# Mixers at 0.25 steps per unit of feed-forward work, and decode rows' second feed-forward products with unsplit weights, in a one-core hybrid decoder layer

## The chip, the cores and the metric

The kernel runs on one core of one Trainium2 chip. The metric is the device time of one execution in microseconds (us). A change of 0.3% of this time is about 8.5 us.

## The reference, cut to what matters

One decoder layer is computed for 2048 prompt rows and for 8 decode rows (one new token of each of 8 sequences), with the same weights. The width is 1024 and the feed-forward width 4096, all in float32.

```
proj = x @ w_in                                   # 1024 -> 3336 columns
o_r  = rwkv7_mix(proj[..., :1792] with token shift)   # recurrent over rows
o_m  = mamba2_mix(rest of proj)                       # scan over chunks of rows
h    = layer_norm(ALPHA * x + concat(o_r, o_m) @ w_out)
ff   = square(relu(h @ w_ff1)) @ w_ff2
y    = layer_norm(ALPHA * h + ff)
```

Besides y, the recurrent states after the last row are returned. What the change touches is the product with `w_ff2` for the 8 decode rows, and when the two mixers (`o_r`, `o_m`) of a block of prompt rows are worked on.

## The kernel before

The prompt is cut into four blocks of 512 rows. Nothing of the mixers of a block can start before its projection, and the output projection of a block needs the block's mixer output `s_o`, which goes through device memory. The 8 decode rows ride along with block 1 (`sblk`).

**Precision.** Large products are not done in plain float32. Each operand is split in two (`split`): ScalarE writes a rounded high part, VectorE (at some places GpSimd) the rest, and `mm3` does three products (high by high, high by low, low by high) of the type `float32r`, lines L166 to L168. Weights come in pieces of 128x512 floats by `wpiece`: a DMA on the SP queue (L205) into a raw buffer of the pool `wr` (7 buffers), then the split into a buffer of the pool `w` (8 buffers). Small products, `mm` at L152, are often done on plain float32 operands; one such product appears in the trace as two matmul instructions.

**Stages.** First the projections of blocks 0 to 3 (`project`), with the mixers of block 0 as filling work at `RATE_M0`. Then `tail(b)` for each block: output projection (16 steps, each yielding 2.6 units), layer norm and transposes, then eight groups of feed-forward work. A group is four calls of `ff1` (24 matmuls of 512 columns each, yielding 5.2 units; they run four ahead of their group, `LA`) and eight second products (12 matmuls each, yielding 2.6). In the last group, `before_last` first finishes whatever filling work is left, then loads `s_o` of block b+1 (`load_o`, L323), its residual rows (L1289, into tiles of the pool `g4`) and the `w_out` pieces, and runs the whole output projection of block b+1; only after that come the second products of the last group.

**Filling work.** `drive` runs a tail and, for every unit that the tail yields, credits the mixers of the next block with `rate` steps; each full credit runs one step of the generator `mixers`, whose work takes 71 steps. From the first `ff1` to the point where the last group starts, a tail yields 32 x 5.2 + 7 x 20.8 = 312 units. `tail(0)` carries the mixers of block 1 and then the decode rows' own mixer work (`sample`) at `RATE_S`; `tail(1)` and `tail(2)` carry the mixers of blocks 2 and 3 at `RATE_M`; `tail(3)` carries none. The last three steps of `mixers` contain the end of `rwkv_post` for the last 128 rows: `inv_root` (step 69), whose four products write 32 output partitions each of one PSUM tile; a round trip of the result through device memory (`bcast_rs`, L552 and L554); the load of `s_bv` (L785); a product with `gup`; and the store of `s_o` (L798) in step 71.

**Order.** The program gives every instruction its buffers and a rank in order of the text above; a list scheduler then fixes one order per engine and for the SP queue, and the engines run it strictly in that order. So a DMA issue on SP that waits for a buffer holds up those behind it.

**Decode rows in the second product.** In `tail(1)`, each of the 8 groups has two halves of 512 output columns. When a half's four weight pieces are loaded, the eight decode rows' products are done first: `hid[f][2]` holds the high and the low part of the hidden values side by side, 16 columns, and eight `float32r` products (four pieces, high and low weight part) accumulate in 16 partitions of one PSUM bank. ScalarE copies them out (L1415) and VectorE adds them to rows 64 to 79 of the tile `hs[4]` (L1416). At the end `fold16` adds high and low rows by a small product.

Of the kernel before, what the change touches and what calls it, by code (L numbers as in the profile page):

```python
# [9 lines left out]
F32 = mybir.dt.float32  # L10
F32R = mybir.dt.float32r
I32 = mybir.dt.int32
AF = mybir.ActivationFunctionType
ALU = mybir.AluOpType
# [9 lines left out]
LA = 4  # L24

TURN = (0, 0, 0, 0, 2, 2, 2, 2)
RATE_M0, RATE_M, RATE_S = 0.2, 0.23, 0.35
BUFS = (("wr", 7), ("w", 8), ("act", 8), ("g4", 13), ("r", 2), ("blk", 4),
        ("m2", 3), ("q2", 2), ("m4", 2), ("ms", 1), ("lr", 1), ("sc", 2), ("ar", 2), ("bk", 1), ("xs", 3),
        ("xf", 1), ("uv", 2), ("bt", 1), ("st", 2), ("r1", 1), ("hids", 8))  # L30
D = 1024
# [2 lines left out]
NS = 8  # L34
# [34 lines left out]
_n = 0  # L69
for _name, _w in (  # L70
    ("ident", 128), ("scm", 128), ("m1", 64), ("m2", 64), ("bm", 4), ("d16", 16), ("tri", 128),
    ("b64", 128), ("cen", 128), ("s16", 8), ("sel", 32), ("one", 2),
):
    CCOL[_name] = (_n, _w)
    _n += _w
# [3 lines left out]
def shape_constants():  # L79
    c = np.zeros((128, NCON), np.float32)  # L80

    def put(name, v):
        o, w = CCOL[name]
        c[:, o:o + w] = v

    p = np.arange(128)
    s = p % 64
    t = np.arange(64)
    put("ident", np.eye(128))
    scm = np.zeros((128, 128))  # L90
    scm[:, :64] = s[:, None] < t[None, :]
    scm[:, 64:] = s[:, None] <= t[None, :]
    put("scm", scm)
    tb, sb = s // 16, t // 16
    put("m1", (tb[:, None] % 2 == 1) & (sb[None, :] == tb[:, None] - 1))
    put("m2", (tb[:, None] >= 2) & (sb[None, :] < 2))
    put("bm", tb[:, None] == np.arange(4)[None, :])
    put("d16", (p % 16)[:, None] == np.arange(16)[None, :])
    put("tri", p[:, None] <= p[None, :])
    blk = (p[:, None] // 64) == (p[None, :] // 64)  # L100
    put("b64", blk)
    put("cen", np.eye(128) - blk / 64.0)
    put("s16", p[:, None] % 8 == np.arange(8)[None, :])
    put("sel", (p[:, None] // 64) == (np.arange(32) % 2)[None, :])
    put("one", 1.0)
    return c


class K:
# [88 lines left out]
        nc.scalar.activation(hi, raw, AF.Copy)  # L198
        (eng or nc.vector).tensor_tensor(out=lo, in0=raw, in1=hi.bitcast(F32), op=ALU.subtract)  # L199

    def wpiece(self, src, shape, tag="w"):

        n = int(np.prod(shape))
        raw = self.sb(tag + "r", (128, 512))
        self.nc.sync.dma_start(raw[:, :n], src)  # L205
        hl = self.sb(tag, (128, 2, 512), F32R)
        self.npiece += 1
        r = {"a": POOLA, "o": POOLO, "f": POOLF}[self.pf]
        pool = r and self.npiece % r == 0
        self.split(raw[:, :n], hl[:, 0, :n], hl[:, 1, :n], self.nc.gpsimd if pool else None)  # L210
        return [hl[:, i, :n].rearrange("p (a b) -> p a b", a=shape[0]) for i in range(2)]
# [20 lines left out]
    def setup_mix(self):  # L232

        tc, nc, A = self.tc, self.nc, self.A
# [48 lines left out]
        c = lambda n, s: self.mp.tile(list(s), F32, name=n)  # L283

        self.wup = []
        for i in range(2):
            raw = self.sb("wr", (128, 512))
# [14 lines left out]
        self.hist = c("hist", (128, 8, 3))  # L302
        nc.gpsimd.memset(self.hist, 0.0)
        self.prl = c("prl", (128, 14))
        self.cen = self.mp.tile([128, 128], F32R, name="cen")
        nc.scalar.activation(self.cen, self.con("cen"), AF.Copy)
        self.b64 = self.mp.tile([128, 128], F32R, name="b64")
        nc.scalar.activation(self.b64, self.con("b64"), AF.Copy)
        self.hst = c("hst", (128, 8, 64))
        nc.gpsimd.memset(self.hst, 0.0)  # L310
        self.ST = self.sb("st", (128, 4, 64))
# [220 lines left out]
    def inv_root(self, groups, ones, scale, eps, clip=False):  # L532


        nc = self.nc
        n = 32 * len(groups)
        pss = self.ps("a" if clip else "m", (128, 128))
        for g, x in enumerate(groups):
            self.mm(pss[32 * g:32 * g + 32, :], ones, x)
        ss, y, t = (self.smp.tile([128, 128], F32, tag=x, name=self.nm(x), bufs=2)[:n] for x in ("rss", "rsy", "rst"))  # L540
        if clip:
            nc.vector.tensor_scalar(out=ss, in0=pss[:n], scalar1=eps, scalar2=None, op0=ALU.max)
        else:
            nc.vector.tensor_scalar(out=ss, in0=pss[:n], scalar1=scale, scalar2=eps, op0=ALU.mult, op1=ALU.add)
        return self.rsqrt(ss, 128, n, (y, t))
# [390 lines left out]
    def sample(self):  # L936
        self.pf = "s"
        nc, A = self.nc, self.A
# [36 lines left out]
        w = V6[:, 1]  # L975
# [18 lines left out]
        tt(sq, kk, kk, M)  # L994
        yield
        pn = self.ps("m", (128, 32))
        self.mm(pn, self.con("b64"), f(sq))
        ss = t(32)
        nc.vector.tensor_scalar(out=ss, in0=pn, scalar1=1e-24, scalar2=None, op0=ALU.max)
        rs = self.rsqrt(ss, 32)  # L1000
# [8 lines left out]
        rk = t(4, 8)  # L1009
# [1 line left out]
        tt(rk, rk, V6[:, 2], M)  # L1011
        yield
        pb = self.ps("m", (128, 32))
        self.mm(pb, self.con("b64"), f(rk))
        bv = t(4, 8)
        tt(bv, pb.rearrange("p (a b) -> p a b", a=4), v, M)

# [63 lines left out]
        y = yield from from_rows(yq)  # L1081
        yield
        pc = self.ps("m", (128, 32))
        self.mm(pc, self.con("cen"), f(y))
        nc.vector.tensor_copy(f(y), pc)
        tt(sq, y, y, M)
        yield
        pv = self.ps("m", (128, 32))
        self.mm(pv, self.con("b64"), f(sq))
        ts(ss, pv, 1.0 / 64, LNX_EPS)  # L1090
        tt(f(y), f(y), self.rsqrt(ss, 32), M)
        tt(y, y, bc("lnw", 4, 8), M)
# [155 lines left out]
                nc.vector.scalar_tensor_tensor(out=h[:, s], in0=h[:, s], scalar=rs, in1=b, op0=ALU.mult, op1=ALU.add)  # L1248
            nc.sync.dma_start(out[:, s], h[:, s])

    def ln_s(self, xs):

        bs = self.sm("bss", [128, 2, 6], bufs=1)[0:8]
        self.fold16(xs)
        for q in range(2):
            self.stats(xs[0:8], bs, q)
        yield from self.ln([xs[0:8]], [bs], 8)

    def fold16(self, xs):

        s16, x = xs[64:80], xs[0:8]
        for q in range(2):
            p = self.ps("b")
            self.mm(p[0:8, :], self.con("s16", 64, 80), s16[:, q * 512:(q + 1) * 512])
            self.nc.vector.scalar_tensor_tensor(out=x[:, q * 512:(q + 1) * 512], in0=x[:, q * 512:(q + 1) * 512],
                                                scalar=ALPHA, in1=p[0:8, :], op0=ALU.mult, op1=ALU.add)

# [11 lines left out]
    def tail(self, b, act, before_last):  # L1279
# [42 lines left out]
                    if kh:  # L1322
                        nc.scalar.activation(xs[64:80, ds_], pss[4][0:16], AF.Copy)
        if smp:
            for _ in self.ln_s(xs):
                pass
        yield 0

# [42 lines left out]
        for g in range(NFT // 4):  # L1371
# [23 lines left out]
            for j, (dh, i) in enumerate(order):  # L1395
                if last and nxt is not None:
                    self.pf = "o"
                    for _ in range(TURN[j]):
                        next(nxt)
                    self.pf = "f"  # L1400
                ds_ = slice(dh * 512, dh * 512 + 512)
                if len(w2s) == dh:
                    w2 = [self.wpiece(A["w_ff2"][f * 128:(f + 1) * 128, ds_], (1, 512)) for f in range(4 * g, 4 * g + 4)]
                    w2s.append(w2)
                    if smp:
                        ps = self.bank()
                        for f in range(4):
                            for s in range(2):
                                self.mm(ps[0:16], hid[f][2], w2[f][s][:, 0, :], f == 0 and s == 0, f == 3 and s == 1)
                        s16 = hs[4][64:80, ds_]  # L1410
                        if g == 0:
                            nc.scalar.activation(s16, ps[0:16], AF.Copy)
                        else:
                            t16 = self.sb("r", (128, 512))[64:80]
                            nc.scalar.activation(t16, ps[0:16], AF.Copy)  # L1415
                            nc.vector.tensor_tensor(out=s16, in0=t16, in1=s16, op=ALU.add)  # L1416
                w2 = w2s[dh]
                ps = self.bank()
                for f in range(4):
                    l = [hid[f][0][:, s, i * 128:(i + 1) * 128] for s in range(2)]  # L1420
                    r = [w2[f][s][:, 0, :] for s in range(2)]
                    self.mm3(ps, l, r, f == 0, f == 3)
                self.accum(hs[i][:, ds_], ps, g == 0)
                if last:
                    self.stats(hs[i], bs[:, i], dh)
                    if nxt is None and dh == 1:
                        if i == 0:
                            ab = self.affine(2)
                        self.norm(hs[i], bs[:, i], ab, rows[i], POOLN[i])
                yield 2.6  # L1430

        def finish():
            if nxt is not None:
                ab = self.affine(2)
                yield from self.ln(hs[:4], [bs[:, i] for i in range(4)], 128)
                for i in range(4):
                    yield from self.gain(hs[i], 128, *ab, rows[i])
            if smp:
                yield from self.ln_s(hs[4])
                yield from self.gain(hs[4][0:8], 8, *ab, A["y_s"])  # L1440

        if nxt is not None:
# [3 lines left out]
    def ff1(self, f, hT, segs, hid=None):  # L1446
# [6 lines left out]
        for o, m in segs:  # L1453
# [8 lines left out]
            c = min(m, TB - o)  # L1462
            self.split(rl[:, :c], hl[:, 0, o:o + c], hl[:, 1, o:o + c])
            if c < m:
                hid[2] = self.sb("hids", (128, 2 * NS), F32R)
                self.split(rl[:, c:m], hid[2][:, 0:NS], hid[2][:, NS:2 * NS])
        return hid


# [88 lines left out]
def layouts(x):  # L1558
# [2 lines left out]
    g = {n: np.asarray(a) for n, a in x.items()}  # L1561
    d = {}
    d["consts"] = shape_constants()

    def cols(name, tiles=None):
        a = g[name].reshape(-1)
# [66 lines left out]
```

## Time and profile before

| | |
|---|---|
| median of 3 runs | 2832.1 us (2827.39 to 2836.89) |
| the profiled execution's own time | 2837.96 us |
| its span, first to last instruction | 2836.1 us |
| mean granted TensorE clock | 0.983 |
| busy share: TensorE matmul, VectorE, ScalarE, GpSimd | 97%, 70%, 44%, 10% |

A busy share is an average over stages. TensorE is the engine that the kernel keeps busy, and its idle time and its clock are what the following rows look at: the busy time of each engine in a stretch, the clock that was granted there, and the chain of instructions that ended last.

### The profile page before, as it was taken

The numbers are of one execution on the slowest core, as the hardware profiler recorded it, in microseconds if no ns is written. First come the engines' busy times: TensorE is split into PE (matmuls) and PEld (weight loads), VectorE is DVE, ScalarE is ACT, GpSimd is POOL, SyncE is SP. The second block draws the span as 40 slices with busy tenths as digits, with TensorE's granted clock in tenths as the row PEclk, the third lists the DMA queues.
The fourth block names the chain that finished last, engine by engine and source line by source line (L and its number), as shares of the span: only waits on it lengthen the run. The fifth ranks groups of instructions, "written<-read, shape, count | busy, mean of one in ns | idle before, by whom it ended". The sixth has DMA issues, their size and how long they took to land.

```text
span 2836.1 us, 49575 instructions
## 1 busy us (share of the span) xinstructions
PE 2739.1 (97%) x17978; PEld 2211.4 (78%) x17978; DVE 1990.6 (70%) x4733; ACT 1246.6 (44%) x2376; POOL 297.0 (10%) x468
## 2 busy tenths in 40 slices
PE   9999999899999999999999999989999997999997
PEld 7788887677776777877888888867777775888886
DVE  7878979868868777774886666558776764664446
ACT  5554544445525443343644444326343332543332
POOL 2222222122210000001000000010000001000001
PEclk9999999999999999999999999989999998999999
DMA  6654655555633444354443343163444334342332
GB/s 203 185 181 138 182 174 143 167 169 166 184 116 121 143 134 136 105 158 155 134 136 113 106 125 114 57 198 130 121 127 127 115 97 139 98 149 88 98 97 71
DMA packets 326841, 382.79 MB, mean 135 GB/s; under 512 B 84222, under 2 KB 190292, under 8 KB 326588
## 3 DMA queue, kind: packets, MB, share of 16 engines
q1 hardware_dynamic: 326596, 379.63, 44.3%
q8 instruction: 141, 2.31, 0.3%
q14 instruction: 104, 0.85, 0.1%
HBM read 318.76 MB, written 60.81 MB: 134 GB/s over the span
## 4 chain that ended last, share of the span: by engine, by line
PE 66%; DVE 5%; DMA 3%; issue 1%; ACT 1%; SPq 0%; POOL 0%; DVEq 0%; ACTq 0%; POOLq 0%
PE psb L166 14%; PE psb L167 14%; PE psb L168 14%; PE psm L152 5%; PE psa L166 4%; PE psa L167 4%; PE psa L168 4%; PE psc L152 2%; PE psm L173 1%; PE psy L751 1%; PE psb L152 1%; DMA wr<-in_w_out_dram 1%; DMA q<-s_bv 0%; DMA g<-in_ln_g_dram 0%; DVE g L1228 0%
## 5 line engine op out<-in xcount | busy, mean ns | idle before, releaser
L198 ACT ACTIVATE w<-wr 128x512 fp32r<-128x512 f32 x788 | 485.5, 626 | 637.9 <-PE psb L168 396.2
L199 DVE TENSOR_TENSOR w<-wr,w 128x512 fp32r<-128x512 f32 x704 | 491.3, 705 | 252.9 <-ACT w L198 248.9
L166 PE MATMUL psb<-act,w 128*128 128x512 f32 (+2 forms) x1688 | 612.4, 363 | 6.8 <-ACT act L198 5.8
L167 PE MATMUL psb<-act,w 128*128 128x512 f32 (+2 forms) x1688 | 605.9, 359 | 0.0
L168 PE MATMUL psb<-act,w 128*128 128x512 f32 (+2 forms) x1688 | 603.3, 357 | 2.1 <-DVE w L199 2.1
L166 PEld LDWEIGHTS psb<-act,w 128*128 128x128 f32 x1688 | 319.6, 189 | 60.1 <-ACT act L198 5.8
L168 PEld LDWEIGHTS psb<-act,w 128*128 128x128 f32 x1688 | 319.2, 189 | 51.3 <-DVE w L199 2.5
L167 PEld LDWEIGHTS psb<-act,w 128*128 128x128 f32 x1688 | 320.0, 190 | 47.0 <-DVE act L199 0.9
L166 PE MATMUL psb<-w,g 128*128 128x512 f32 x768 | 310.0, 404 | 1.0 <-DVE g L1510 1.0
L167 PE MATMUL psb<-w,g 128*128 128x512 f32 x768 | 305.5, 398 | 0.0
L168 PE MATMUL psb<-w,g 128*128 128x512 f32 x768 | 304.6, 397 | 0.0
L1510 DVE TENSOR_TENSOR g<-psb,g 128x512 f32<-128x512 f32 x168 | 115.4, 687 | 104.2 <-PE psb L168 103.8
L166 PEld LDWEIGHTS psb<-w,g 128*128 128x128 f32 x768 | 144.7, 188 | 38.7 <-issue 2.0
L199 POOL TENSOR_TENSOR w<-wr,w 128x512 fp32r<-128x512 f32 x84 | 118.3, 1409 | 538.8 <-ACT w L198 256.4
L168 PEld LDWEIGHTS psb<-w,g 128*128 128x128 f32 x768 | 144.8, 189 | 33.7 <-issue 0.2
L167 PEld LDWEIGHTS psb<-w,g 128*128 128x128 f32 x768 | 144.9, 189 | 32.2 <-issue 0.4
L1460 ACT ACTIVATE r<-psb 128x512 f32<-128x512 f32 (+2 forms) x120 | 61.6, 513 | 182.2 <-PE psb L168 180.4
L199 DVE TENSOR_TENSOR g<-r,g 128x512 fp32r<-128x512 f32 (+1 forms) x160 | 92.5, 579 | 57.1 <-ACT g L198 56.7
L166 PE MATMUL psa<-act,w 128*128 128x512 f32 (+1 forms) x320 | 114.1, 357 | 0.0
L167 PE MATMUL psa<-act,w 128*128 128x512 f32 (+1 forms) x320 | 112.6, 352 | 0.0
L168 PE MATMUL psa<-act,w 128*128 128x512 f32 (+1 forms) x320 | 112.4, 351 | 0.0
L166 PE MATMUL psb<-g,w 128*128 128x256 f32 (+2 forms) x312 | 105.4, 338 | 0.3 <-ACT g L578 0.3
(380 smaller groups left out, 4886.2 us busy)
## 6 DMA issues: line engine op xcount, KB each, us to landing
wr<-in_w_ff_dram SPq DMA_DIRECT2D x512, 256.0 KB
wr<-in_w_in_dram SPq DMA_DIRECT2D x208, 256.0 KB
lr<-d_l SPq DMA_DIRECT2D x256, 64.0 KB
wr<-in_w_out_dram SPq DMA_DIRECT2D x64, 256.0 KB
s_m<-g SPq DMA_DIRECT2D x48, 256.0 KB
ms<-s_m SPq DMA_DIRECT2D x16, 768.0 KB
wr<-in_xT_dram SPq DMA_DIRECT2D x32, 256.0 KB
s_ar<-g SPq DMA_DIRECT2D x16, 512.0 KB
```

Source lines behind the costliest of these rows:

```text
L152: return self.nc.tensor.matmul(out, l, r, start=start, stop=stop)
L166: nc.tensor.matmul(out, l[0], r[0], start=first, stop=False)
L167: nc.tensor.matmul(out, l[0], r[1], start=False, stop=False)
L168: nc.tensor.matmul(out, l[1], r[0], start=False, stop=last)
L173: self.nc.tensor.transpose(out, in_, self.cst[p0:p0 + k, o + p0:o + p0 + k])
L198: nc.scalar.activation(hi, raw, AF.Copy)
L199: (eng or nc.vector).tensor_tensor(out=lo, in0=raw, in1=hi.bitcast(F32), op=ALU.subtract)
L751: acc = lambda o, l, r, start, stop: nc.tensor.matmul(o, l, r, start=start, stop=stop, skip_group_check=True)
L1460: nc.scalar.activation(rl, ps, AF.Relu)
L1510: self.nc.vector.tensor_tensor(out=h, in0=ps, in1=h, op=ALU.add)
```

## The change

Five things are edited.

1. `RATE_M` goes from 0.23 to 0.25, so the mixers of blocks 2 and 3 get a step every 4 units of feed-forward work in `tail(1)` and `tail(2)`.
2. The decode rows' second products use the raw float32 weights (`raws`) and plain float32 hidden values (32 columns, of which 8 are filled and 24 are zero). The four products of a half write the four groups of 32 partitions of one PSUM bank, without accumulation. The raw buffers are now read by TensorE too.
3. The sums of the halves are kept in a tile `acc4` of its own (128 partitions, from the pool `g4`); VectorE adds the PSUM bank to it directly, and `fold` sums the four groups at the end with a 128-row constant.
4. The pool `g4` gets 14 buffers instead of 13; the scratch tile `rst` of `inv_root` gets 1 instead of 2.
5. Two 128x128 constants leave the table `consts` and come by a DMA of their own through a `wr` buffer during setup.

```diff
-RATE_M0, RATE_M, RATE_S = 0.2, 0.23, 0.35
-BUFS = (("wr", 7), ("w", 8), ("act", 8), ("g4", 13), ("r", 2), ("blk", 4),
+RATE_M0, RATE_M, RATE_S = 0.2, 0.25, 0.35
+BUFS = (("wr", 7), ("w", 8), ("act", 8), ("g4", 14), ("r", 2), ("blk", 4),
...
+    put("s32", p[:, None] % 32 == np.arange(8)[None, :])
...
-    def wpiece(self, src, shape, tag="w"):
+    def wpiece(self, src, shape, tag="w", raws=None):
...
         raw = self.sb(tag + "r", (128, 512))
         self.nc.sync.dma_start(raw[:, :n], src)
+        if raws is not None:
+            raws.append(raw)
...
+        raw = self.sb("wr", (128, 512))[:, :256]
+        nc.sync.dma_start(raw, A["consts2"])
+        self.b64 = self.mp.tile([128, 128], F32R, name="b64")
+        nc.scalar.activation(self.b64, raw[:, 0:128], AF.Copy)
         self.cen = self.mp.tile([128, 128], F32R, name="cen")
-        nc.scalar.activation(self.cen, self.con("cen"), AF.Copy)
-        self.b64 = self.mp.tile([128, 128], F32R, name="b64")
-        nc.scalar.activation(self.b64, self.con("b64"), AF.Copy)
+        nc.scalar.activation(self.cen, raw[:, 128:256], AF.Copy)
...
-        ss, y, t = (self.smp.tile([128, 128], F32, tag=x, name=self.nm(x), bufs=2)[:n] for x in ("rss", "rsy", "rst"))
+        ss, y, t = (self.smp.tile([128, 128], F32, tag=x, name=self.nm(x), bufs=n_)[:n]
+                    for x, n_ in (("rss", 2), ("rsy", 2), ("rst", 1)))
...
-    def fold16(self, xs):
+    def fold(self, xs, parts, sel):
...
-            self.mm(p[0:8, :], self.con("s16", 64, 80), s16[:, q * 512:(q + 1) * 512])
+            self.mm(p[0:8, :], sel, parts[:, q * 512:(q + 1) * 512])
...
-                    w2 = [self.wpiece(A["w_ff2"][f * 128:(f + 1) * 128, ds_], (1, 512)) for f in range(4 * g, 4 * g + 4)]
+                    raws = []
+                    w2 = [self.wpiece(A["w_ff2"][f * 128:(f + 1) * 128, ds_], (1, 512), raws=raws)
+                          for f in range(4 * g, 4 * g + 4)]
                     w2s.append(w2)
                     if smp:
+
+                        if g == 0 and dh == 0:
+                            acc4 = self.wide()
                         ps = self.bank()
                         for f in range(4):
-                            for s in range(2):
-                                self.mm(ps[0:16], hid[f][2], w2[f][s][:, 0, :], f == 0 and s == 0, f == 3 and s == 1)
-                        s16 = hs[4][64:80, ds_]
+                            self.mm(ps[32 * f:32 * f + 32], hid[f][2], raws[f])
                         if g == 0:
-                            nc.scalar.activation(s16, ps[0:16], AF.Copy)
+                            nc.scalar.activation(acc4[:, ds_], ps, AF.Copy)
                         else:
-                            t16 = self.sb("r", (128, 512))[64:80]
-                            nc.scalar.activation(t16, ps[0:16], AF.Copy)
-                            nc.vector.tensor_tensor(out=s16, in0=t16, in1=s16, op=ALU.add)
+                            nc.vector.tensor_tensor(out=acc4[:, ds_], in0=ps, in1=acc4[:, ds_], op=ALU.add)
...
-                yield from self.ln_s(hs[4])
+                yield from self.ln_s(hs[4], acc4, self.con("s32"))
...
-                hid[2] = self.sb("hids", (128, 2 * NS), F32R)
-                self.split(rl[:, c:m], hid[2][:, 0:NS], hid[2][:, NS:2 * NS])
+                hid[2] = self.sb("hids", (128, 32))
+                nc.gpsimd.memset(hid[2], 0.0)
+                nc.scalar.activation(hid[2][:, 0:NS], rl[:, c:m], AF.Copy)
```

## Rows read from the trace of the kernel before

**Rows 1.** The page: busy time and share of each engine, with instruction counts.
```profile
PE 2739.1 (97%) x17978; PEld 2211.4 (78%) x17978; DVE 1990.6 (70%) x4733; ACT 1246.6 (44%) x2376; POOL 297.0 (10%) x468
```

**Rows 2.** Stretches of 100 us: busy us and count per engine, granted clock, DMA.
```profile
core 0: us, PE busy (x) PEld busy (x) DVE busy (x) ACT busy (x) POOL busy (x), PEclk, DMA share, GB/s
1000.00:1100.00 100.00, 99.90 (x857) 77.46 (x856) 77.47 (x232) 37.63 (x76) 5.46 (x10) 1.00 0.46 135
...
1800.00:1900.00 100.00, 91.12 (x585) 74.43 (x586) 49.29 (x92) 33.88 (x71) 13.64 (x10) 0.91 0.40 123
...
2300.00:2400.00 100.00, 80.53 (x528) 62.16 (x525) 52.42 (x124) 32.70 (x58) 6.40 (x5) 0.90 0.38 116
...
2500.00:2600.00 100.00, 100.00 (x433) 80.98 (x432) 50.61 (x71) 38.97 (x67) 0.00 (x0) 1.00 0.32 102
```

**Rows 3.** The same view, of the three boundaries between tails.
```profile
1278.00:1288.00 10.00, 5.07 (x16) 3.86 (x15) 7.59 (x16) 2.94 (x6) 0.00 (x0) 0.67 0.79 260
1851.00:1876.00 25.00, 16.12 (x80) 12.13 (x79) 16.62 (x27) 10.10 (x18) 4.59 (x4) 0.66 0.86 290
2372.00:2398.00 26.00, 6.98 (x19) 4.75 (x20) 10.52 (x15) 10.66 (x17) 3.87 (x4) 0.61 0.83 261
```

**Rows 4.** The chain that ended last, 2355 to 2400 us: start, length, what.
```profile
2358.32 0.36 PE psm L152 x8
...
2367.25 0.89 PE psm L152 x8
...
2370.01 0.25 PE psb L168
2370.26 0.36 SPq L1289
2370.72 5.44 DMA q<-s_bv
...
2377.72 2.29 DMA s_o<-q
...
2385.84 5.13 DMA wr<-in_w_out_dram
...
2391.68 0.79 PE psb L166
```

**Rows 5.** The same chain, 1836 to 1880 us.
```profile
1837.47 0.36 PE psm L152 x8
1837.83 1.94 PE psb L152 x8
...
1849.47 0.25 PE psb L168
...
1872.58 0.79 PE psb L167
```

**Rows 6.** Issues on the SP queue, 1180 to 1330 us: start, length, line, count.
```profile
1280.81 0.38 SPq L1289 DMA_DIRECT2D g<-in_x_p_dram  x1
1281.25 2.30 SPq L205 DMA_DIRECT2D wr<-in_w_out_dram  x4
...
1305.73 1.71 SPq L1289 DMA_DIRECT2D g<-in_x_p_dram  x3
```

**Rows 7.** Waits of TensorE, 1200 to 1330 us: total, times, longest.
```profile
PE psm L173 <- DMA m<-d_y: 4.9, 1, 4.9
```

**Rows 8.** TensorE in order of time, 1821.6 to 1824.3 us.
```profile
1821.95 2.02 PE L152 MATMUL psb<-w,hids 128*16 128x512 f32 x8
1823.81 0.39 PE L166 MATMUL psb<-w,g 128*128 128x512 f32 x1
```

**Rows 9.** Issues on the SP queue, 1420 to 1560 us.
```profile
1447.46 4.82 SPq L650 DMA_DIRECT2D d_l<-sc  x8
1452.69 3.65 SPq L655 DMA_DIRECT2D lr<-d_l  x8
```

**Rows 10.** The page, costliest groups: busy us, mean ns, idle before and releaser.
```profile
L1510 DVE TENSOR_TENSOR g<-psb,g 128x512 f32<-128x512 f32 x168 | 115.4, 687 | 104.2 <-PE psb L168 103.8
```

More of the change, by code (lines that the diff above doesn't have):

```diff
@@ L71 @@
     ("ident", 128), ("scm", 128), ("m1", 64), ("m2", 64), ("bm", 4), ("d16", 16), ("tri", 128),
-    ("b64", 128), ("cen", 128), ("s16", 8), ("sel", 32), ("one", 2),
+    ("s16", 8), ("sel", 32), ("one", 2), ("s32", 8),
 ):
@@ L99, in shape_constants @@
     put("tri", p[:, None] <= p[None, :])
-    blk = (p[:, None] // 64) == (p[None, :] // 64)
-    put("b64", blk)
-    put("cen", np.eye(128) - blk / 64.0)
     put("s16", p[:, None] % 8 == np.arange(8)[None, :])
@@ L105, in shape_constants, with head_constants @@
     put("one", 1.0)
+    put("s32", p[:, None] % 32 == np.arange(8)[None, :])
     return c
+def head_constants():
+    p = np.arange(128)
+    blk = ((p[:, None] // 64) == (p[None, :] // 64)).astype(np.float32)
+    return np.concatenate([blk, np.eye(128, dtype=np.float32) - blk / 64.0], 1).astype(np.float32)
 class K:
@@ L996, in sample @@
         pn = self.ps("m", (128, 32))
-        self.mm(pn, self.con("b64"), f(sq))
+        self.mm(pn, self.b64.bitcast(F32), f(sq))
         ss = t(32)
@@ L1013, in sample @@
         pb = self.ps("m", (128, 32))
-        self.mm(pb, self.con("b64"), f(rk))
+        self.mm(pb, self.b64.bitcast(F32), f(rk))
         bv = t(4, 8)
@@ L1083, in sample @@
         pc = self.ps("m", (128, 32))
-        self.mm(pc, self.con("cen"), f(y))
+        self.mm(pc, self.cen.bitcast(F32), f(y))
         nc.vector.tensor_copy(f(y), pc)
@@ L1088, in sample @@
         pv = self.ps("m", (128, 32))
-        self.mm(pv, self.con("b64"), f(sq))
+        self.mm(pv, self.b64.bitcast(F32), f(sq))
         ts(ss, pv, 1.0 / 64, LNX_EPS)
@@ L1249, in norm, with ln_s @@
             nc.sync.dma_start(out[:, s], h[:, s])
-    def ln_s(self, xs):
+    def ln_s(self, xs, parts, sel):
         bs = self.sm("bss", [128, 2, 6], bufs=1)[0:8]
-        self.fold16(xs)
+        self.fold(xs, parts, sel)
         for q in range(2):
@@ L1257, in ln_s @@
         yield from self.ln([xs[0:8]], [bs], 8)
-    def fold16(self, xs):
-        s16, x = xs[64:80], xs[0:8]
+    def fold(self, xs, parts, sel):
+        x = xs[0:8]
         for q in range(2):
             p = self.ps("b")
-            self.mm(p[0:8, :], self.con("s16", 64, 80), s16[:, q * 512:(q + 1) * 512])
+            self.mm(p[0:8, :], sel, parts[:, q * 512:(q + 1) * 512])
             self.nc.vector.scalar_tensor_tensor(out=x[:, q * 512:(q + 1) * 512], in0=x[:, q * 512:(q + 1) * 512],
@@ L1324, in tail @@
         if smp:
-            for _ in self.ln_s(xs):
+            for _ in self.ln_s(xs, xs[64:80], self.con("s16", 64, 80)):
                 pass
@@ L1563, in layouts @@
     d["consts"] = shape_constants()
+    d["consts2"] = head_constants()
     def cols(name, tiles=None):
```

## The prediction

> **What bounds the kernel now.** I read the page first. TensorE is busy 97% of the span, the next engine 70% [rows 1], so time can be won where TensorE stands still, where its clock is low, or by giving it less to do. The second view, busy time in stretches of 100 us, says where it stands still. The reader is to see that a feed-forward stretch has none of it, with mixers beside it (99.90 of 100 us, at the faster pace `RATE_S`) or without (100.00 us, 433 matmuls, so 0.231 us each), while the stretches in which one tail hands over to the next lose 9 and 19 us and show a mean clock of 0.91 and 0.90 [rows 2]. The third view is the same one, close to the three boundaries. A mean clock between 0.5 and 1 there is a mixture of the two levels, 1.2 and 2.4 GHz; busy time times that clock is roughly the work done at full speed. Boundary `tail(1)` to `tail(2)`: 25 us long, 16.12 busy at 0.66, so 10.6 us of work and 14.4 lost. Boundary `tail(2)` to `tail(3)`: 26 - 6.98 x 0.61 = 21.7 lost. Boundary `tail(0)` to `tail(1)`: 10 - 5.07 x 0.67 = 6.6 lost [rows 3], but that one ends on a round trip of the decode rows' mixer (`d_y`) [rows 7], whose pace `RATE_S` is not touched.
>
> The fourth view, the chain that ended last, says what the other two wait for. At 2370.26 the feed-forward work of group 6 ends on TensorE; then come `q<-s_bv`, the store of `s_o`, its load back, a `w_out` piece and its split, and at 2391.68 the first product of the output projection [rows 4]. So the mixers finish too late: not for lack of any engine's time, but because their last steps stand near the end of the tail and a row of round trips follows. Boundary 1 shows the same chain [rows 5].
>
> **The pace.** Step n of the mixers runs at the first yield at which the units so far reach n / rate. At 0.23, step 69 (`inv_root`) needs 300 units and runs at 301.6, 10.4 units before the 312 at which group 7 starts. A step of 2.6 units is 12 matmuls x 0.231 = 2.77 us [rows 2], so this should be 4 x 2.77 = 11.1 us before the end; the trace has 2370.26 - 2358.32 = 11.9 us, and the `gup` products of step 71 stand 3.0 us before it [rows 4] against 2.8 worked out. TensorE's order thus follows the program's, and the same sum can be made for 0.25: step 69 needs 276 units and runs at 280.8, 31.2 units or 33.3 us before the end. The whole end of the mixers moves 22.2 us earlier.
>
> From `inv_root` to the first product of the output projection the chain takes 2391.68 - 2358.32 = 33.4 us at boundary 2 [rows 4] and 1872.58 - 1837.47 = 35.1 us at boundary 1 [rows 5]. Feed-forward work of 33.3 us now lies beside it. The holes of 2391.68 - 2370.26 = 21.4 us [rows 4] and 1872.58 - 1849.72 = 22.9 us [rows 5] shrink to about zero, and the chain should become a little shorter too, since the residual loads (L1289) that stand before `q<-s_bv` on SP wait for the end of group 6 and no longer precede it. What is late next? The residual loads themselves, which need `g4` tiles, and the `w_out` pieces. Boundary 0, where the mixers are done long before, shows the order: one residual load, then four `w_out` pieces, and three more residual loads 24 us later [rows 6]. So the pieces are not kept behind the residual. I leave 2 us lost at each boundary for what is not in place. Gain: 14.4 + 21.7 - 4 = 32 us. Upper bound 36. Lower bound: if the `w_out` pieces are still requested only at the end of group 6, each boundary keeps a landing of 5.13 us [rows 4], a split, and a first stretch at the low clock, about 10 us in all; the gain is then 16. I take 32, since boundary 0 is the nearest case.
>
> The price of the faster pace is a denser mixture, 71 steps in 284 units rather than 309. `tail(0)` runs a step every 2.9 units with TensorE busy 99.90 of 100 us [rows 2], so nothing is charged.
>
> **The decode rows' products.** Removed: 16 sets of eight `float32r` products. A set takes from 1821.95 to the next matmul at 1823.81, 1.86 us [rows 8]. Added: 16 sets of four plain float32 products, eight matmul instructions of 512 columns. No such set is in the trace, but two near ones are. Four float32 products with the full 128 stationary columns and 128 moving columns (`gup`) take 0.89 us; four with 32 stationary columns each, into four groups of 32 partitions (`inv_root`), also with 128 moving columns, take 0.36 us [rows 4]. The second kind is the form of the new set, and it overlaps; what differs is 512 columns. If four run fully side by side, 512 columns cost what one of them costs, four times a quarter of 0.89, so 0.89 us; if the whole 0.36 us grows with the columns, 1.44 us. I take 1.0, nearer the first, as 0.36 exceeds 0.89 / 4 by 0.14 us and an overhead does not grow with columns. Saved per set 0.86 us, in 16 sets 13.8 us (bounds 6.7 and 15.5). They lie in `tail(1)`, where TensorE sets the time, so the saving counts in full.
>
> Here a rule of the Trainium skill speaks against the change: "FP8 and Floating Point Precision", section TensorE Precision Notes, says that true float32 takes four passes through the array. By that rule a set of four passes a piece replaces two products a piece, and would take twice 1.86, 3.7 us, which makes the kernel 30 us longer, unless passes of different column groups run at once; the 0.36 against 0.89 us above says that they do.
>
> **Costed at nothing.** VectorE's add grows from 16 to 128 partitions of the same 512 columns, and a PSUM add of that shape costs 0.687 us [rows 10]; fourteen ScalarE copies go. Both engines have room beside a busy TensorE (77 and 38 of 100 us) [rows 2], and four banks turn over while one is read. The clearing of 32 small tiles falls to GpSimd, busy 10% [rows 1]. `rst` is written and read by VectorE alone, in its order, so one buffer makes no new wait between engines. The constants are the same bytes in two loads, needed well after the first projections. The 14th `g4` buffer is taken by `acc4` from `tail(1)` into `tail(2)`, and elsewhere gives one tile more; I allow 5 us either way for a schedule shuffled by these.
>
> **The raw buffers** are the one edit with a real wait in it. Four of the seven `wr` buffers now stay taken until TensorE reaches the set, where earlier the split freed them. The fourth piece of a half can be requested only when the half before starts on TensorE, and has 4 x 2.77 = 11.1 us until it is needed; a landing of 5.13 us and two splits make some 6.5 us [rows 4, 10]. That is covered. Behind a waiting raw load on SP stand the mixers' own loads, and before it may stand a burst of 16 issues, 8.5 us long [rows 9].
>
> **Rivals.**
>
> *A, as worked out.* Gain 32 + 14 = 46 us. The profiled execution (2838 us, a span of 2836.1 and 2 us around it) would become 2792; it lies 6 us above the median of 2832, so the median becomes 2786. Its own range, by the bounds, 2774 to 2798. Chance 0.62.
>
> *B, a new wait takes part of the holes' place* (`w_out` pieces, or the residual rows late). Gain 16 + 14 = 30: 2802, and down to 2809 with the dear set. For it speaks that the cover equals the chain to within 2 us; against it, boundary 0. Chance 0.20.
>
> *C, the four products do not run side by side at 512 columns.* A set costs four times 0.89, 3.56 us, so 16 sets add 16 x 1.70 = 27 us and 2832 - 32 + 27 = 2827 results: no change. Against it stands the pair 0.36 and 0.89 us. A part of it would appear where the scheduler puts a mixer's matmuls between the four. Chance 0.09.
>
> *D, the held raw buffers starve the feed-forward, slower than before.* If a burst of 8.5 us precedes the fourth piece, 8.5 + 6.5 = 15.0 us stand against 11.1, and TensorE waits 3.9 us in that half. `tail(1)` has nine such bursts and 16 halves: nine hits cost 35 us, leaving 2821. It turns slower by 0.3% only when 14 of the 16 halves are hit, (46 + 8.5) / 3.9. That takes some other delay on SP too. Chance 0.09, of which 0.07 slower.
>
> **Numbers.** 0.3%, 8.5 us, is about what a measurement can tell from no change. A, B and 0.04 of C and D are faster: 0.86; the rest of C is no change: 0.07; slower 0.07. Predicted is A's 2786. The range 2773 to 2811 holds A and B; C and D, 0.18, are left out.
>
> **What the changed profile would show.** The stretches at both later boundaries with TensorE busy over 90% and the clock at 1; `s_o<-q` issued some 14 us before group 6 ends, not 7 after; sets of eight 512-column matmuls of 32 stationary columns lasting about 1.0 us; `tail(1)` about 14 us shorter between boundaries. The prediction is wrong if the sets last over 1.9 us, if a hole of more than 5 us stays at a boundary, or if new TensorE waits on `w` splits appear inside `tail(1)`.

## The result

| | before | after |
|---|---|---|
| median | 2829.96 us (4 runs, 2827.39 to 2836.89) | 2788.58 us (4 runs, 2787.33 to 2791.17) |
| the profiled execution's own time, and its span | 2837.96, 2836.1 us | 2789.01, 2787.2 us |
| mean granted TensorE clock | 0.983 | 0.991 |

The ratio is 0.9846, with a 95% interval from 0.9832 to 0.9859: faster, by 41 us between the medians and 44 by the ratio, where 46 were forecast. 2788.58 stands 2.6 us above the predicted 2786 and inside the range.

**The boundaries.** These are two stretches of 100 us of the changed kernel. They answer to those in which `tail(1)` and `tail(2)` hand over [rows 2], now at about 1839 and 2344 us.

```profile
core 0: us, PE busy (x) PEld busy (x) DVE busy (x) ACT busy (x) POOL busy (x), PEclk, DMA share, GB/s
...
1800.00:1900.00 100.00, 100.00 (x510) 80.14 (x509) 60.81 (x124) 40.92 (x72) 12.17 (x8) 1.00 0.40 133
...
2300.00:2400.00 100.00, 100.00 (x444) 80.86 (x443) 54.68 (x113) 40.21 (x65) 11.58 (x8) 1.00 0.41 136
```

TensorE, which was busy 91 and 81 us of 100, is busy all the time, and the clock stays at 1. The SP queue shows why. These are its issues around the second of the two boundaries (start, length, line, count):

```profile
2321.64 0.35 SPq L796 DMA_DIRECT2D q<-s_bv  x1
2322.05 0.89 SPq L1300 DMA_DIRECT2D g<-in_x_p_dram  x2
2327.56 0.38 SPq L809 DMA_DIRECT2D s_o<-q  x1
2329.76 5.17 SPq L333 DMA_DIRECT2D wr<-s_o  x8
2335.21 5.50 SPq L210 DMA_DIRECT2D wr<-in_w_out_dram  x6
2342.28 1.02 SPq L1300 DMA_DIRECT2D g<-in_x_p_dram  x2
2343.39 11.72 SPq L210 DMA_DIRECT2D wr<-in_w_out_dram  x10
```

And these are TensorE's matmuls at the end of group 6 and the start of the output projection:

```profile
2309.54 0.43 PE L157 MATMUL psm<-q,cst 128*32 128x128 f32 x8
...
2343.93 0.39 PE L173 MATMUL psb<-w,g 128*128 128x512 f32 x1
2344.16 0.40 PE L171 MATMUL psb<-w,act 128*128 128x512 f32 x1
```

`s_o<-q` is issued at 2327.56, 16.6 us before the output projection starts; before, it came some 7 us after the end of group 6 [rows 4]. `q<-s_bv` no longer stands between the residual loads, six `w_out` pieces are requested ahead of the last two residual loads, as at the boundary of `tail(0)` [rows 6], and the first product of the output projection follows the last of group 6 after 0.23 us. From `inv_root` (2309.54) to that product 34.6 us pass, nearly all of it feed-forward work. The first `w_out` split is ScalarE's row

```profile
2339.64 1.27 ACT L203 ACTIVATE w<-wr 128x512 fp32r<-128x512 f32 x2
```

Its first piece is done at half of this row, 2340.3 us. So the chain from `inv_root` to it takes 30.7 us here and ends 3.9 us before the product that needs it: it became shorter, as forecast, and lies wholly beside feed-forward work.

**The decode rows' products.** TensorE in order of time at one set of the changed kernel, which answers to [rows 8]:

```profile
1814.36 1.06 PE L157 MATMUL psb<-wr,hids 128*32 128x512 f32 x8
1815.36 0.50 PE L171 MATMUL psb<-w,g 128*128 128x512 f32 x1
1815.70 0.40 PE L172 MATMUL psb<-w,g 128*128 128x512 f32 x1
```

The set takes 1815.36 - 1814.36 = 1.00 us, as forecast, instead of 1.86. The matmul behind it is followed after 0.34 us rather than 0.23: an additional 0.1 us that the old sets did not have (0.24 at 1823.81 to 1824.05 in the kernel before). The four groups are not its cause, since full-width float32 products are followed by it too. Behind `gup` in the changed kernel it is 0.31 us:

```profile
2315.57 1.05 PE L157 MATMUL psm<-qsg,gup 128*128 128x128 f32 x8
2316.38 0.47 PE L171 MATMUL psb<-act,w 128*128 128x512 f32 x1
2316.69 0.39 PE L172 MATMUL psb<-act,w 128*128 128x512 f32 x1
```

### The profile page after: what moved, and what is told of

It reads as the page before. It is cut to its first block, busy times and chain, and to the rows that moved or that the text cites. A ratio compares the mean times of both kernels' runs of the same rounds, so it can differ in the third digit from the quotient of the medians.

```text
span 2787.2 us, 49564 instructions
## 1 busy us (share of the span) xinstructions
PE 2720.8 (98%) x17978; PEld 2196.0 (79%) x17978; DVE 1980.5 (71%) x4701; ACT 1240.4 (45%) x2362; POOL 299.6 (11%) x500
## 5 line engine op out<-in xcount | busy, mean ns | idle before, releaser
L173 PEld LDWEIGHTS psb<-w,g 128*128 128x128 f32 x768 | 144.9, 189 | 34.3 <-issue 0.8
```

What stands on the lines that cost most here:

```text
L173: nc.tensor.matmul(out, l[1], r[0], start=False, stop=last)
```

## The experiments

Each kernel was timed in five rounds against the kernel before; ratios are to that.

| run | what | ratio (95%) |
|---|---|---|
| e1_rate_only | before, pace 0.25 | 0.9889 (0.9875 to 0.9902) |
| e2_decode_only | after, pace 0.23 | 0.9954 (0.9941 to 0.9966) |
| e3_small_edits | before, small edits alone | 0.9974 (0.9964 to 0.9983) |
| e4_rate_024 | after, pace 0.24 | 0.9902 (0.9889 to 0.9916) |
| e5_rate_030 | after, pace 0.30 | 0.9859 (0.9844 to 0.9874) |
| e6_one_group | after, products in one group | 0.9981 (0.9969 to 0.9994) |
| e7_wr_5 | after, 5 raw buffers | 0.9978 (0.9968 to 0.9987) |
| e8_rate_s_040 | after, decode pace 0.40 | 0.9869 (0.9856 to 0.9883) |
| e9_small_g4_13 | before, small edits, 13 `g4` | 0.9988 (0.9976 to 1.0) |
| e10_old_sets | after, old products | 0.9886 (0.9866 to 0.9905) |
| e11_together | after, sets tied together | 0.9843 (0.9824 to 0.9863) |

**The pace alone.**

```diff
-RATE_M0, RATE_M, RATE_S = 0.2, 0.23, 0.35
+RATE_M0, RATE_M, RATE_S = 0.2, 0.25, 0.35
```

> The kernel before with RATE_M 0.25 and nothing else. Theory (the pace moves the end of the mixers 22 us earlier and that closes both holes): 32 to 36 us shorter, a ratio near 0.988, and TensorE busy over 95% in the stretches where tail(1) and tail(2) end. Rival 1 (the 14th g4 buffer lets the residual loads go early and that closed the holes): with 13 buffers holes of 8 us or more stay and the gain is under 20 us. Rival 2 (the gain came from the products): ratio near 1.

1.11% of the 2834.28 us that the kernel before took beside it is 31.5 us, and the interval goes from 28 to 35: just under the theory's 32 to 36, and 0.5 us below the prediction's 32. Rival 1 falls, since this kernel has 13 `g4` buffers and no hole. Its two boundaries, by busy time, each in the 26 us before the output projection starts:

```profile
1821.00:1847.00 26.00, 26.00 (x114) 19.88 (x112) 16.10 (x26) 13.43 (x25) 3.98 (x3) 1.00 0.72 220
2331.00:2357.00 26.00, 26.00 (x113) 20.96 (x112) 15.99 (x24) 12.95 (x23) 2.26 (x2) 1.00 0.64 209
```

**Everything but the pace**, the changed kernel with

```diff
-RATE_M0, RATE_M, RATE_S = 0.2, 0.25, 0.35
+RATE_M0, RATE_M, RATE_S = 0.2, 0.23, 0.35
```

> The changed kernel with RATE_M back at 0.23. Theory: the two holes of some 20 us return, and only the cheaper sets (16 times about 0.76 us with the slower start of the matmul behind them) remain: 9 to 14 us shorter than before, ratio near 0.996. Rival (the 14th buffer or the schedule closed the holes): ratio under 0.990.

0.46%, 13 us, and both holes are back:

```profile
1835.00:1860.00 25.00, 14.08 (x81) 11.10 (x80) 13.60 (x22) 9.82 (x18) 3.49 (x3) 0.66 0.77 260
2353.00:2379.00 26.00, 7.31 (x36) 4.42 (x35) 10.32 (x15) 10.42 (x19) 2.50 (x2) 0.62 0.73 237
```

The rows are almost those of the kernel before [rows 3]. The pace is what closed the holes, and the two gains add: 0.9889 x 0.9954 = 0.9844 against 0.9846 for both.

**A pace between**, the same line with 0.24.

> The changed kernel with RATE_M 0.24. Step 69 then needs 287.5 units, runs at 291.2, 20.8 units or 22.2 us before group 7, against a chain of 33 to 35 us. Theory (the cover must reach the chain): holes of 11 to 13 us stay at both boundaries, and the time is 15 to 25 us above the changed kernel, near 2807. Rival (any pace a little above 0.23 does, the wait was one late issue on SP): no more than 5 us above the changed kernel.

2805.74 us against 2807 expected. The chain that ended last shows the hole that is left at the second boundary:

```profile
2326.73 0.36 PE psm L157 x8
...
2344.80 2.19 DMA s_o<-q
2347.01 0.33 SPq L333
2347.39 3.28 DMA wr<-s_o
...
2353.09 6.87 DMA wr<-in_w_out_dram
2359.98 0.64 ACT w L203
```

The `inv_root` at 2326.73 is followed by the first `w_out` split's end at 2360.62, 33.9 us later; the feed-forward work beside it lasted to 2350.2, 23.5 us (22.2 worked out), and no feed-forward work was left for the rest. So at this boundary the hole shrinks with the cover, step by step (at 0.23 20.9 us in the kernel before and 19.3 in e2_decode_only, 10.5 at 0.24, none at 0.25); the rival, one late issue that any faster pace repairs, falls.

At the first of the two boundaries, `tail(1)` to `tail(2)`, the same sum does not come out. TensorE, and in one row ScalarE, in order of time there:

```profile
1807.63 0.43 PE L157 MATMUL psm<-q,cst 128*32 128x128 f32 x8
...
1833.13 0.40 PE L173 MATMUL psb<-w,g 128*128 128x512 f32 x1
...
1838.72 0.66 PE L178 MATMUL psm<-cst,ms 128*128 128x128 f32 x4 [4.10 <-DVE sc L657]
...
1844.44 3.28 ACT L203 ACTIVATE w<-wr 128x512 fp32r<-128x512 f32 x5 [1.36 <-DMA wr<-in_w_out_dram]
...
1848.04 1.97 PE L157 MATMUL psm<-m,m 128*128 128x256 f32 x4
1849.56 1.15 PE L171 MATMUL psb<-w,act 128*128 128x512 f32 x3
```

The cover is 25.7 us (1807.63 to 1833.36), but 41.9 us pass from `inv_root` to the output projection, so 16.2 us of hole stay where 11 to 13 were expected. Two things differ. The first `w_out` split is done at 1845.1 (a fifth of ScalarE's row), 37.5 us after `inv_root` and not 33 to 35. And the output projection starts only 4.5 us later, right behind products of the mixers (`psm`) that stand ahead of it in TensorE's order and had waited for VectorE (4.10 us in the row shown). So a second chain ends this hole, which the prediction does not have. Why both were late was not shown; at 0.25 nothing is left of either.

**A pace far above**, 0.30.

> The changed kernel with RATE_M 0.30: the mixers end some 50 units earlier still. Theory (once the cover reaches the chain nothing more is to be had): within 4 us of the changed kernel, near 2789, and no holes. Rival (the denser mixture costs TensorE time): 5 to 15 us longer, with more idle time inside tail(1) and tail(2).

The ratio is 0.13% above that of the changed kernel, inside both intervals: nothing more is won, and no loss to the denser mixture can be told from the noise.

**One group of partitions instead of four.**

```diff
-                            self.mm(ps[32 * f:32 * f + 32], hid[f][2], raws[f])
+                            self.mm(ps[0:32], hid[f][2], raws[f], f == 0, f == 3)
...
-                yield from self.ln_s(hs[4], acc4, self.con("s32"))
+                yield from self.ln_s(hs[4], acc4[0:32], self.con("s32", 0, 32))
```

> The changed kernel with the four float32 products of a set accumulated in one group of 32 partitions instead of four groups, so that they can't run side by side; same operands and columns. Theory (the saving is the running side by side): a set lasts 3.4 to 3.6 us instead of 1.0, 16 sets 38 to 42 us, near 2829. Rival (the products are bound by reading the columns or by issue, and the groups don't matter): within 8 us of the changed kernel.

2829.57 us, against some 2829 expected; by the ratios the one group costs 1.35%, 38 us. TensorE in order of time at one set:

```profile
1442.81 3.62 PE L157 MATMUL psb<-wr,hids 128*32 128x512 f32 x8
1446.37 0.50 PE L171 MATMUL psb<-w,g 128*128 128x512 f32 x1
```

3.56 us for the same eight instructions, the figure that the prediction's rival C had worked out, against 1.00 in four groups. One product of 512 columns takes 3.56 / 4 = 0.89 us here, and 0.23 as a `float32r` product: 3.9 times. The four passes that the Trainium skill gives a true float32 product ("FP8 and Floating Point Precision", TensorE Precision Notes) agree with it. In four groups the same work is 3.6 times as fast. Of putting small outputs into column groups of their own, the Trainium skill ("TensorE: Matmul & The Clock Gate", Part 3: Packing small matmuls — row/col tiling) says that the span is that of one matmul and about 4 ns for each further tile. One product alone takes 0.97 us here (1771.87 to 1772.84 in the rows shown with e11_together), so an estimate with the 4 ns of that page is 0.98 us for four; the measured 1.00 us agrees.

**Five raw buffers.**

```diff
-BUFS = (("wr", 7), ("w", 8), ("act", 8), ("g4", 14), ("r", 2), ("blk", 4),
+BUFS = (("wr", 5), ("w", 8), ("act", 8), ("g4", 14), ("r", 2), ("blk", 4),
```

> The changed kernel with 5 raw weight buffers instead of 7, so one is left beside the four that a set holds. Theory (the seven leave more room than tail(1) needs): the stretch of tail(1) grows by under 5 us, other stages by a few us, near 2795. Rival D (held raw buffers starve the feed-forward): tail(1) grows by 20 us or more, more than the stretch of tail(2), which holds none.

The time grew by 1.32%, 37 us by the ratios, but not where rival D said. Busy time by stage (projections, `tail(0)`, `tail(1)`) with five buffers:

```profile
0.00:799.00 799.00, 753.06 (x5100) 613.65 (x5101) 644.92 (x1495) 401.25 (x751) 178.29 (x344) 0.99 0.58 167
799.00:1333.00 534.00, 512.07 (x3374) 398.43 (x3373) 380.14 (x962) 220.94 (x410) 31.52 (x40) 0.97 0.44 132
1333.00:1873.00 540.00, 533.60 (x4268) 445.88 (x4267) 366.32 (x946) 241.43 (x548) 34.55 (x65) 1.00 0.39 122
```

and with seven, in the changed kernel:

```profile
0.00:783.00 783.00, 750.65 (x5099) 613.21 (x5100) 643.78 (x1500) 404.19 (x758) 176.01 (x346) 0.99 0.58 173
783.00:1300.00 517.00, 504.17 (x3375) 394.43 (x3374) 378.60 (x958) 215.71 (x403) 30.69 (x38) 0.98 0.44 134
1300.00:1839.00 539.00, 535.10 (x4268) 447.39 (x4267) 369.66 (x948) 244.06 (x552) 37.75 (x67) 0.99 0.39 123
```

`tail(1)`, where the sets hold four of the buffers, takes 540 us instead of 539; the projections lose 16 us and `tail(0)` 17, where no set holds any. With one free buffer left beside the four the feed-forward still does not starve, so D is refuted with room to spare. The three stages together hold all of the 34 us by which the span of the profiled execution grew (2821.6 us against 2787.2). My expectation for the whole, near 2795, was wrong: with five buffers TensorE waits in the projections for splits of `w`,

```profile
PE psb L171 <- ACT w L203: 8.3, 4, 4.1
```

a wait that the changed kernel does not have there.

**The decode rows' mixers, faster.**

```diff
-RATE_M0, RATE_M, RATE_S = 0.2, 0.25, 0.35
+RATE_M0, RATE_M, RATE_S = 0.2, 0.25, 0.4
```

> The changed kernel with RATE_S 0.40 instead of 0.35, so the mixers of block 1 and the decode rows' mixers end earlier in tail(0). Theory (the hole left at the first boundary is of the same kind, work that ends too near the end): the wait on d_y goes and 4 to 6 us are won, near 2784. Rival (that hole is set by the decode rows' own chain, whatever the pace): no change.

Nothing was won. The ratio is 0.23%, 6 us, above that of the changed kernel, and the two intervals only just overlap. TensorE's waits from 1200 to 1330 us in this run:

```profile
PE psm L178 <- DMA m<-d_y: 6.5, 1, 6.5
```

The wait is 4.4 us in the changed kernel (4.9 in the kernel before [rows 7]). It grew although the steps came earlier: these are the store of `d_y` and the product that waits for it, first in the changed kernel, then in this run.

```profile
1269.87 1.09 SPq L1080 DMA_DIRECT2D d_y<-lr  x2
1276.04 0.38 PE L178 MATMUL psm<-cst,m 8*128 8x8 f32 x4 [4.37 <-DMA m<-d_y]
...
1264.58 1.09 SPq L1080 DMA_DIRECT2D d_y<-lr  x2
1273.26 0.56 PE L178 MATMUL psm<-cst,m 8*128 8x8 f32 x4 [6.49 <-DMA m<-d_y]
```

The store is issued 5.3 us earlier, the product starts only 2.8 us earlier. So the hole at the boundary of `tail(0)` looks like the others, but an earlier start moves its end by half as much. What holds that chain was not settled.

**The small edits**: `g4`, `rst` and the constants, with the old pace and the old products, once with 14 and once with 13 `g4` buffers.

```diff
...
-        ss, y, t = (self.smp.tile([128, 128], F32, tag=x, name=self.nm(x), bufs=2)[:n] for x in ("rss", "rsy", "rst"))
+        ss, y, t = (self.smp.tile([128, 128], F32, tag=x, name=self.nm(x), bufs=n_)[:n]
+                    for x, n_ in (("rss", 2), ("rsy", 2), ("rst", 1)))
...
```

> The kernel before with the 14th g4 buffer, one rst buffer and the constants in two loads, but the old pace and the old sets. Theory: within 5 us of before, holes unchanged. Rival (more buffers help the projections or the boundaries): 10 us or more shorter. Rival (one rst buffer hurts the mixers): 5 us or more longer.

> The small edits alone (one rst buffer, the constants in two loads) with 13 g4 buffers, old pace and old sets. Against before, the same edits with 14 buffers took 0.9974 of the time. Theory (the 14th g4 buffer gave those 7 us): no change against before, ratio 0.999 to 1.001. Rival (the constants' loads or the reshuffled order gave them): ratio 0.996 to 0.998 with 13 buffers as well.

With 14 buffers 0.26%, 7 us, more than the 5 allowed; with 13, 0.12% and an interval that ends at 1.0. The two intervals overlap, so whether the 14th buffer gave the difference stays open.

**The changed kernel with the old products**, their 16-column operands and their sums.

```diff
-                            self.mm(ps[32 * f:32 * f + 32], hid[f][2], raws[f])
+                            for s in range(2):
+                                self.mm(ps[0:16], hid[f][2], w2[f][s][:, 0, :], f == 0 and s == 0, f == 3 and s == 1)
...
```

> The changed kernel with the decode rows' old split products: the pace 0.25 and the small edits stay. Theory (the sets save TensorE time, which counts in full once no hole is left to take it up): 10 to 13 us longer than the changed kernel, near 2801. Rival (the sets are worth the 7 us that they gave at pace 0.23): near 2796.

2800.16 us and a ratio of 0.9886: the products are worth 0.40%, 11 us, here. In the traces the sets, each from its start to the next matmul and the parts of cut sets added, sum to 30.6 us with the old products and 18.8 us in the changed kernel; less the 0.1 us behind each new set some 10 us are saved. Its ratio is that of the pace alone (0.9889), so at the new pace the small edits are worth nothing that shows.

**The sets tied together.**

```diff
-                        for f in range(4):
-                            self.mm(ps[32 * f:32 * f + 32], hid[f][2], raws[f])
+                        prev = self.mm(ps[96:128], hid[3][2], raws[3])
+                        for f in (0, 1, 2):
+                            with self.tc.high_priority(RANK), self.tc.issue_after(prev.ins):
+                                prev = self.mm(ps[32 * f:32 * f + 32], hid[f][2], raws[f])
```

> The changed kernel with the four products of a set tied together in TensorE's order, the one whose weights land last first, so that no mixer products come between them. Three of the 16 sets were cut in the changed kernel, which kept each in the array for one or two passes more (0.8 to 1.3 us each). Theory: 2 to 4 us shorter, near 2785, all 16 sets at 1.0 us. Rival (the tie keeps mixers' products waiting or makes TensorE wait for the last weights): no gain or longer.

In the changed kernel three of the 16 sets were cut by mixers' products, here the one at 1771.87:

```profile
1771.87 1.05 PE L157 MATMUL psb<-wr,hids 128*32 128x512 f32 x2
1772.84 0.56 PE L157 MATMUL psc<-uv,sc 128*64 128x64 f32 x10
1773.34 0.68 PE L157 MATMUL psm<-xs,xs 64*64 64x64 f32 x16
1773.95 0.45 PE L157 MATMUL psc<-uv,sc 128*64 128x64 f32 x6
1774.32 1.06 PE L157 MATMUL psb<-wr,hids 128*32 128x512 f32 x6
```

One product alone costs the whole 1.0 us that four together cost (1771.87 to 1772.84), and so do three (1774.32 to 1775.31, where the next matmul starts). With the tie all 16 sets take 1.0 us, but the ratio (0.9843) is within 0.03% of the changed kernel's: three cuts, some 3 us, are too few to be measured.

## Why the prediction was right

**The pace** was right in mechanism and near in size. Step 69 was to run 33.3 us before group 7 and ran 34.6 us before the output projection; the holes closed fully rather than to 2 us each; 31.5 us came of it alone against 32. That this is so close is luck in part: by the prediction's own sum holes that close fully are worth 36 us. That lies just outside the interval of e1_rate_only (28 to 35), and the two other pairs of runs that differ in the pace alone give 25 us (e3_small_edits and e10_old_sets) and 31 us (e2_decode_only and the changed kernel). So the 4 us that were kept back for holes that stay, and perhaps more, went to something that the sum does not have. What it was stays open; the denser mixture, charged with nothing, is one candidate.

The pace of 0.24 tests the arithmetic by itself. At the second boundary it came out: cover 22.2 us worked out, 23.5 measured, and a chain of 33.9 us that still sticks out by the difference. At the first it did not, since the chain was longer there and a second one ended after it.

**Readings that were off.** For the first boundary the prediction took 1872.58 as the first product of the output projection and 1849.72 as the end of the feed-forward work, both from the chain that ended last. TensorE in order of time in the kernel before:

```profile
1837.40 0.43 PE L152 MATMUL psm<-q,cst 128*32 128x128 f32 x8
...
1851.40 0.40 PE L168 MATMUL psb<-w,g 128*128 128x512 f32 x1
...
1870.56 0.51 PE L166 MATMUL psb<-w,act 128*128 128x512 f32 x1 [2.31 <-ACT w L198]
```

The chain leaves TensorE at the product that released something else, and feed-forward work goes on until 1851.6; and it comes back at a product behind the first one. So the chain is 33.2 us and not 35.1, the hole 18.9 us and not 22.9. The error did no harm, as the cover of 33.3 us was enough for either. Two counts are off as well: rival D's nine bursts in `tail(1)` are eight in the trace, and the bounds of A's own range give 2775 and not 2774 at its lower end.

**What was to be late next** was right too: the `w_out` pieces pass the residual loads. Rival B did not occur.

**The products** had the right mechanism and one term too large. The set measured 1.00 us as taken, and 3.56 in one group, C's price. The saving was put at 0.86 x 16 = 13.8 us, and about 11 came (0.9886 against 0.9846). Not in the sum was the 0.1 us by which the matmul after each set starts its successor later: (0.86 - 0.10) x 16 = 12.2. It could have been read from the kernel before, where the same 0.34 us stand behind `inv_root` (2358.61 to 2358.95). The three cut sets, which rival C foresaw in part, take off some 3 us more, and with the old sets' own cuts the traces leave some 10 us. The runs do not tell this from 11: taken together, the two intervals allow some 4 to 18 us.

That the saving "counts in full" holds only once the holes are closed. At the old pace everything else together gave 13 us, of which the small edits alone had 7 (0.9954 against 0.9974), so the products left some 6. In that run the chain from `inv_root` to the output projection at the first of the two boundaries took 34.3 us against 31.4 in the run of the small edits, and its hole 21.0 us against 17.2. That the hole took up the difference fits these numbers; it was not shown by a run of its own.

**The small edits** were put at nothing, with 5 us either way. At the new pace that is what they were; at the old one they gave 7, for a reason that stays open.

**D** did not occur: inside `tail(1)` of the changed kernel TensorE's longest wait is 3.1 us, before a small product (`psm`), and none is for a split of `w`.

```profile
PE psm L157 <- issue: 3.1, 1, 3.1
```

Even one spare buffer beside the four held ones was enough to keep D off.

## What to carry to other kernels

When filling work runs beside a busy engine and its result is needed at a fixed point, count the latency of the round trips after its last step, and set the pace so that this much of the main work is left when the last step starts; less leaves a hole of the difference or, where other work stands ahead in the engine's order, a longer one; more gives nothing. The pace of a step in a program whose order is fixed can be worked out on paper and checked against two instructions of a trace. Read the start and the end of a hole from the engine's own instructions in order of time, not from the chain that ended last. Plain float32 products with few output rows were cheaper than split ones here because four of them write four groups of 32 partitions at once (1.00 us a set against 1.86); a single one costs as much as the four.

## What the runs showed of the hardware

Four float32 products of 512 columns, each with 32 stationary columns and writing its own 32 partitions of one bank, take 1.00 us together and 3.56 us if they write the same partitions. After such a set the next full-width matmul holds TensorE 0.34 us instead of 0.23; the 16-column `float32r` sets before had no such delay. Plain float32 products of the full width (0.31) and sets in one group (0.33) are followed by it as well, so it goes with plain float32 operands and not with the groups.
